# Where the Strassen weight factors of a down projection are made: in its own stage, or ahead of it and kept in DRAM

## The chip, the cores and the metric

The kernel runs on one core of a Trainium2 chip. The metric is device time in microseconds (us); with one core the slowest core is that core. Three runs of the kernel before gave 1456.2, 1456.57 and 1451.91 us, a median of 1456.2 us.

## What is computed

One step of one decoder layer on 1056 tokens (1024 of a prompt, 32 of eight decode sequences) of 1024 features, in float32. Two token mixers with four heads each come first (an mLSTM and an HGRN2), then an output projection, then a gated feed-forward part and a final norm. The change touches the feed-forward part only:

```python
D_FF = -(-8 * D_MODEL // (3 * 256)) * 256        # 2816
...
x = x + jnp.einsum('btm,md->btd', mix, w_out)
h2 = _rmsnorm(x, norm_ffn)
ff = jax.nn.silu(jnp.einsum('btd,df->btf', h2, w_gate)) * jnp.einsum('btd,df->btf', h2, w_up)
x = x + jnp.einsum('btf,fd->btd', ff, w_down)
...
y_prompt = _rmsnorm(xp, norm_final)
y_sample = _rmsnorm(xs, norm_final)
```

## The kernel before, in words

**Products.** Every float32 matrix product is made of three TensorE (PE) products of parts. An operand is cut into hi (its float32r rounding, a copy by ScalarE, ACT) and lo (the operand minus hi, a subtraction by VectorE, DVE, or GpSimd, POOL). The three products are hi hi, hi lo and lo hi.

**Stages.** After the mixers and the output projection, the feed-forward part has 22 feature tiles of 128. Tiles 0 and 1 are done plainly. The other 20 go through the seven products P1 to P7 of Strassen and Winograd. In the **gate and up products** (line 1229, about 746 to 1162 us of the span) there are 20 units u, each a gate or an up matrix for a pair of feature tiles. A unit has seven steps, a step two column halves j of 12 products with a moving operand of 264 columns. The results are summed by DVE, sent through silu by ACT, multiplied, and stored to a DRAM tensor d_ff (g_store, line 1210). The **plain part** of the down projection (line 1476) follows, to 1185 us, and then the **down stage** proper (d_step, line 1435): five chunks of four feature tiles, and in each chunk four groups, 20 groups g in all. A group is for a pair of output tiles and has seven steps of two times 6 products. After each six, DVE adds the PSUM bank to the output X in SBUF (line 1439). The final norm overlaps with the last chunk.

**Operands of the down stage.** The moving operands of a chunk (B11, T1, T2, B21, B22, T3, T4) are made from d_ff while the chunk before is multiplied (stage1, stage2): loads into three `rg` buffers, sums on DVE (lines 1299 to 1325), casts on ACT (1281), and lo subtractions of 528 columns on POOL (1282). The weights of a group are made by dsplit while the group before is multiplied. A load of 512 KB brings a raw block of `wd` into a `raw` buffer. DVE makes S1 to S4 as four sums of 256 columns (lines 1384, 1385, 1391, 1392). ACT casts, and POOL subtracts for lo, three times with 512 columns and once with 256 (line 1380; for two groups near the end DVE does it). The results go to a ring of five `whi` and five `wlo` buffers.

**What sets the order.** The program is in a hand-written order. Work beside the products is written as generators, and each emitted block of six products calls `hook()`, which counts every generator's wait down by one and runs those that are due. `yield 4` means: go on four hooks later. Each engine and each DMA queue then works through its own instructions in that order. All loads and stores that matter here are issued by one queue, SP's, where a transfer that waits (for a buffer, or for data that is to be stored) holds up those written behind it. In the gate and up products the factors of the gate and up weights are made in the same way by gsplit: sums of 512 columns on DVE (line 1146), casts on ACT (1157), lo on POOL (1158).

**PSUM in a gate or up unit.** The steps come in the order P5(u), P6(u), P1(u+1), P7(u), P2(u+1), P4(u), P3(u). P4 adds to the bank that P7 has left, so DVE must have read P7's result before P4 starts, with P2(u+1) in between. P7 in the same way needs ACT's copy of P6's result, with P1(u+1) in between.

Of the kernel before, what the change touches and what calls it, by code (L numbers as in the profile page):

```python
# [28 lines left out]
NS = 5  # L29
# [11 lines left out]
def hybrid_step(ctx: ExitStack, tc: tile.TileContext, i, o):  # L41
# [156 lines left out]
    def norm_rstd(key, n, acc, w=(2, 3)):  # L198
        """the rstd of n tokens on all partitions, from the squares summed over the feature tiles in acc"""
# [41 lines left out]
    # per-feature constants  # L241
# [7 lines left out]
    def conv_consts():  # L249
        # half the convolution and half the output gate: y sigmoid(y) = (y/2) (tanh(y/2) + 1)  # L250
# [17 lines left out]
    # ---- mLSTM gates  # L268
# [127 lines left out]
    # ---- mLSTM  # L396
# [93 lines left out]
    def norm_cols(s, sqs, nch, d2=None, p=128):  # L490
        """s = (sqs / 128 + EPS * d2) ** -0.5"""
# [108 lines left out]
    def sample_core(h_off, w, vnorm, st_in, decay, out_state, n_io, d2, k_scale, later=None):  # L600
        """the decode sequences of one head group: four heads x 32 tokens on the partitions"""
# [126 lines left out]
    # ---- HGRN2  # L728
# [174 lines left out]
    # ------------------------------------------------------------------ unit list  # L903
# [37 lines left out]
    # output projection; the token order from here on: 1024 prompt tokens, 32 decode tokens  # L941
# [62 lines left out]
    # feed-forward, first NPLAIN feature tiles  # L1004
# [36 lines left out]
    # feed-forward, the other feature tiles: pairs of them (rows of A) times two halves of the tokens (columns of B), the  # L1041
    # contraction in two halves: the seven products of Strassen and Winograd
# [21 lines left out]
    def t_prep():  # L1064
        """T1 = B12 - B11, T2 = B22 - T1, T3 = B22 - B12, T4 = B21 - T2"""
# [46 lines left out]
    WLW, DS0 = (14, 10), 1  # L1112
    DSL, DSM = {"P1": 0, "P2": 1, "P7": 2}, {"P1": 3}
# [23 lines left out]
    def gsplit(g, u, dve=False):  # L1137
        """the factors of the products: A11 A12 | S1 = A21 + A22, S2 = S1 - A11 | S3 = A11 - A21, A22 | S4 = A12 - S2"""
# [52 lines left out]
    def g_out(u, r, th, j, ps, other=None, op=None):  # L1191
        """row tile r, token half th, columns j: ps or ps + other is there"""
# [54 lines left out]
    # down projection: NS times four feature tiles in the same way (the contraction in two pairs of tiles, pairs of output  # L1247
    # tiles, halves of the tokens), the last two tiles plainly
# [3 lines left out]
    def memb(r):  # L1252
        """place r of the ring of operands: hi and lo of two feature tiles, half of the tokens"""
# [18 lines left out]
    def raw_ff(c, f):  # L1272
        """the two column blocks of a feature tile: halves of the tokens, in the last chunk halves of each half"""
# [16 lines left out]
    def stage1(c):  # L1290
        """B11, T1 = B12 - B11, T2 = B22 - T1, B21"""
# [26 lines left out]
    def diffs(c, k):  # L1318
        """T3 = B22 - B12, T4 = B21 - B11 - T3"""
# [7 lines left out]
    def stage2(c):  # L1327
        """B22, T3, T4"""
# [18 lines left out]
    draw, dw = {}, {}  # L1347

    def dload(g):
        if g >= NG:  # L1350
            return
        t = draw[g] = wp.tile([128, 1024], F32, tag="raw", name="raw", bufs=NRAW)
        f = NPLAIN + 4 * (g // 4)
        src = i["wd"].rearrange("(f p) d -> p f d", p=128)[:, f:f + 4, 256 * (g % 4):256 * (g % 4) + 256]
        nc.sync.dma_start(t.rearrange("p (f c) -> p f c", c=256), src)

    def dsplit(g):
        """A11 A12 A22 | S1 = A21 + A22, S2 = S1 - A11, S4 = A12 - S2, S3 = A11 - A21"""
        while g not in draw:
            yield 5  # L1360
        r = draw[g].rearrange("p (f c) -> p f c", c=256)
        a11, a12, a21, a22 = r[:, 0:2, 0:128], r[:, 2:4, 0:128], r[:, 0:2, 128:256], r[:, 2:4, 128:256]

        def pair(j):
            # the weights of the last chunk stay: five tiles in the ring, three in free places of the other ring
            if (g, j) in WPL:
                r = WPL[g, j]
                if r == 6:
                    return t4t[0][:, 0:1024], t4t[0][:, 1056:2080]
                return HI[:, 1056 * r:1056 * r + 1024], LO[:, 1056 * r:1056 * r + 1024]  # L1370
            return [wp.tile([128, 1024], F32R, tag=t, name=t, bufs=NW) for t in ("whi", "wlo")]

        def cut2(t):
            return t.rearrange("p (f c) -> p f c", c=128)

        def put(w, o_, src):
            n = 128 * src.shape[1]
            h, lw = cut2(w[0][:, o_:o_ + n]), cut2(w[1][:, o_:o_ + n])
            nc.scalar.activation(h, src, AF.Copy)
            (nc.vector if g in PUTD else nc.gpsimd).tensor_tensor(lw, src, h.bitcast(F32), op=OP.subtract)  # L1380
        w0 = pair(0)
        put(w0, 0, r[:, :, 0:128])
        sa = cut2(stile(512))
        nc.vector.tensor_tensor(sa[:, 0:2], a21, a22, op=OP.add)  # L1384
        nc.vector.tensor_tensor(sa[:, 2:4], sa[:, 0:2], a11, op=OP.subtract)  # L1385
        dw[g, "P1"], dw[g, "P2"], dw[g, "P4"] = [[x[:, o_:o_ + 256] for x in w0] for o_ in (0, 256, 512)]
        yield 5
        w1 = pair(1)
        put(w1, 0, sa)
        sb = cut2(stile(512))  # L1390
        nc.vector.tensor_tensor(sb[:, 0:2], a12, sa[:, 2:4], op=OP.subtract)  # L1391
        nc.vector.tensor_tensor(sb[:, 2:4], a11, a21, op=OP.subtract)  # L1392
        dw[g, "P5"], dw[g, "P6"], dw[g, "P3"], dw[g, "P7"] = [[x[:, o_:o_ + 256] for x in w1] for o_ in (0, 256, 512, 768)]
        done.add(("ds1", g))
        yield 3
        put(w1, 512, sb)
        yield 1
        put(w0, 512, a22)
        start(dload_late(g + 2), ("dl", g), 6)

    PUTD = (NG - 3, NG - 2)
    WPL = {(NG - 3, 1): 4, (NG - 1, 0): 5, (NG - 1, 1): 6}

    def dload_late(g):
        dload(g)
        return
        yield
# [7 lines left out]
    def d_step(g, p):  # L1415
        """a product for a pair of output tiles, halves of the tokens; in the last chunk for two pairs, the quarters of a half"""
# [27 lines left out]
    # the first NPLAIN feature tiles of the down projection plainly  # L1444
# [50 lines left out]
    def facc(acc, sq, dve, wait=0):  # L1495
        """a generator: acc += sq"""
# [8 lines left out]
    def squares(h):  # L1505
        """the first four tiles, half h of the tokens"""
# [14 lines left out]
    def last_squares(m, q):  # L1521
        """the last four tiles of a quarter, as they are done"""
# [48 lines left out]
    def final_half():  # L1571
        """the first half of the tokens"""
# [20 lines left out]
    # ------------------------------------------------------------------ emission  # L1593
# [88 lines left out]
    for ui, u in enumerate(units + [None]):  # L1682
        if ui == units1:
            start(t3_prep(), ("t3",))
            gi, TPK = 2, 2
            for k, (gu_, p) in enumerate(steps):
# [25 lines left out]
            for m in range(KT):  # L1712
                if m == 0:
                    dload(0)
                    dload(1)
                    load_x2(4)
                    load_x2(6)
                if m == DS0:
                    start(dsplit(0), ("ds", 0))
# [6 lines left out]
            for k, (sl, g, p) in enumerate(dsteps):  # L1726
                c, s_ = g // 4, sl % 28
                need = (g,) if g < LC else (2 * g - LC, 2 * g - LC + 1) if g < LC + 2 else ()
                if p == "P1":
                    for x in need:  # L1730
                        finish(("ds1", x))
                    if g % 4 == 0:
                        finish(("s1", c))
                if p == "P2":
                    for x in need:
                        finish(("ds", x))
                    if g % 4 == 0:
                        finish(("s2", c))
                if p == "P5" and g + 1 < LC:
                    start(dsplit(g + 1), ("ds", g + 1))  # L1740
                if p in DSL and g == LC - 1 or p in DSM and g == LC:
                    x = LC + (DSL[p] if g < LC else DSM[p])
                    start(dsplit(x), ("ds", x))
# [170 lines left out]
```

## Time and profile before

| | |
|---|---|
| runs | 1451.91, 1456.2, 1456.57 us |
| span of the profiled execution, first to last instruction | 1451.2 us |
| time of that execution outside the span | not shown; the fastest run is 0.7 us above the span |
| busy share of PE, DVE, ACT, POOL | 95, 62, 36, 50% |
| loads for the down stage | `rg<-d_ff` 42 times 528 KB, `raw<-in_wd` 22 times 512 KB |
| mean DMA rate over the span | 95 GB/s |

The profile is of one execution, with times in us. PE is TensorE, DVE VectorE, ACT ScalarE, POOL GpSimd, SP the queue that issues DMAs. A name as `S<-raw` is output and input of an instruction by the program's names, and L1384 is line 1384 of the kernel before. A busy PE is not a PE at its peak, because matmuls are pipelined and their ends modelled; a better measure is the number of products in a stretch of time. A GB/s is 10^9 bytes a second, a KB 1024 bytes.

### The profile page before, as it was taken

What the parts mean: (1) busy time and instruction counts of PE and PEld (TensorE: products, weight loads), DVE (VectorE), ACT (ScalarE), POOL (GpSimd) and SP (SyncE); (2) the same over time, 40 slices, a digit from 0 to 9 for tenths busy, and PEclk for the clock granted to TensorE, in tenths of its full rate; (3) what the DMA queues carried; (4) which work ended last, traced back from release to release, by engine and by line L of the source; (5) the groups of instructions that cost most, each with busy time, mean ns of one, the idle gap of its engine ahead of it and who ended that gap; (6) DMA issues with size and microseconds to landing.
All of it is one profiled execution on the core that took longest, in us unless ns stands there. A gap on an engine that the chain in (4) does not pass through costs nothing. (4 is left out here: it accounts for less than half of the span.)

```text
span 1451.2 us, 26916 instructions
## 1 busy us (share of the span) xinstructions
PE 1376.6 (95%) x10384; PEld 1339.6 (92%) x10384; DVE 904.0 (62%) x2120; ACT 528.8 (36%) x1195; POOL 731.9 (50%) x720
## 2 busy tenths in 40 slices
PE   7879999999999999999989999999999999998886
PEld 7769999999999998899989999999999998888885
DVE  7876657666776767745472233233322389999986
ACT  6554433322222223223344343333334423333343
POOL 5313213234343435223456655656555778888854
PEclk9989999999999999999999999999999999999998
DMA  6012212320010114443542222222212563334303
GB/s 216 22 42 76 64 37 86 109 79 29 33 44 18 44 32 133 142 148 119 182 139 74 82 89 89 69 72 89 89 64 69 182 235 134 134 134 145 123 30 121
DMA packets 85833, 138.54 MB, mean 95 GB/s; under 512 B 8240, under 2 KB 61000, under 8 KB 85192
## 3 DMA queue, kind: packets, MB, share of 16 engines
q1 hardware_dynamic: 85272, 136.57, 28.7%
q8 instruction: 82, 1.34, 0.4%
q14 instruction: 47, 0.39, 0.1%
q10 hardware_dynamic: 432, 0.24, 0.1%
HBM read 107.03 MB, written 29.75 MB: 94 GB/s over the span
## 5 line engine op out<-in xcount | busy, mean ns | idle before, releaser
L135 PE MATMUL mm<-HI,whi 128*128 128x384 f32 (+2 forms) x1160 | 382.7, 330 | 6.9 <-ACT gA L302 2.9
L137 PE MATMUL mm<-HI,wlo 128*128 128x384 f32 (+2 forms) x1160 | 363.8, 314 | 1.3 <-POOL wlo L97 1.3
L136 PE MATMUL mm<-LO,whi 128*128 128x384 f32 (+2 forms) x1160 | 363.9, 314 | 0.7 <-DVE LO L961 0.4
L135 PEld LDWEIGHTS mm<-HI,whi 128*128 128x128 f32 x1160 | 222.2, 192 | 12.2 <-ACT gA L302 3.2
L136 PEld LDWEIGHTS mm<-LO,whi 128*128 128x128 f32 x1160 | 222.4, 192 | 1.7 <-DVE LO L961 0.6
L137 PEld LDWEIGHTS mm<-HI,wlo 128*128 128x128 f32 x1160 | 221.9, 191 | 1.8 <-POOL wlo L97 1.8
L97 POOL TENSOR_TENSOR wlo<-raw,whi 128x512 fp32r<-128x512 f32 x90 | 119.7, 1339 | 144.1 <-ACT whi L96 99.2
L1158 POOL TENSOR_TENSOR wlo<-S,whi 128x512 fp32r<-128x512 f32 x78 | 107.0, 1373 | 87.1 <-ACT whi L1157 85.8
L1229 PE MATMUL mx<-T,whi 128*128 128x264 f32 x640 | 118.2, 284 | 0.0
L1229 PEld LDWEIGHTS mx<-T,whi 128*128 128x128 f32 x640 | 99.0, 188 | 0.0
L802 POOL TENSOR_TENSOR ck<-ck,wib 128x192 f32<-128x192 f32 (+2 forms) x72 | 41.2, 572 | 100.6 <-PE mx L757 56.2
L1229 PE MATMUL mx<-HI,whi 128*128 128x264 f32 x320 | 91.0, 284 | 0.0
L1229 PE MATMUL mx<-T,wlo 128*128 128x264 f32 x320 | 90.9, 284 | 0.0
L1229 PE MATMUL mx<-HI,wlo 128*128 128x264 f32 x320 | 90.9, 284 | 0.0
L1229 PE MATMUL mx<-LO,whi 128*128 128x264 f32 x320 | 90.7, 283 | 0.0
L1282 POOL TENSOR_TENSOR LO<-rg,HI 128x528 fp32r<-128x528 f32 x52 | 78.4, 1514 | 10.5 <-ACT HI L1281 5.8
L1435 PE MATMUL mx<-HI,whi 128*128 128x264 f32 x208 | 62.3, 300 | 9.9 <-DVE X L1439 9.9
L1157 ACT ACTIVATE whi<-S 128x512 fp32r<-128x512 f32 x80 | 50.2, 629 | 58.4 <-DVE S L1146 58.4
L1229 PE MATMUL mm<-HI,wlo 128*128 128x264 f32 x240 | 68.2, 284 | 0.0
L1229 PE MATMUL mm<-HI,whi 128*128 128x264 f32 x240 | 68.2, 284 | 0.0
L1229 PE MATMUL mm<-LO,whi 128*128 128x264 f32 x240 | 67.9, 283 | 0.0
L1439 DVE TENSOR_TENSOR X<-X,mx 128x264 f32<-128x264 f32 x160 | 60.7, 418 | 8.2 <-PE mx L1435 8.2
(544 smaller groups left out, 3751.8 us busy)
## 6 DMA issues: line engine op xcount, KB each, us to landing
rg<-d_ff SPq DMA_DIRECT2D x42, 528.0 KB
raw<-in_wA SPq DMA_DIRECT2D x31, 512.0 KB
raw<-in_wgu SPq DMA_DIRECT2D x24, 512.0 KB
raw<-in_wd SPq DMA_DIRECT2D x22, 512.0 KB
d_ff<-sg SPq DMA_DIRECT2D x40, 264.0 KB
rg<-in_wgu SPq DMA_DIRECT2D x20, 512.0 KB
d_h<-X SPq DMA_DIRECT2D x4, 1056.0 KB
X<-d_x SPq DMA_DIRECT2D x4, 1056.0 KB
```

Source lines behind the costliest of these rows:

```text
L97: (nc.gpsimd if pool else nc.vector).tensor_tensor(lo[:, s], raw[:, s], hi[:, s].bitcast(F32), op=OP.subtract)
L135: nc.tensor.matmul(ps[:, :n], wh, rh[:, k, :], start=(k == 0), stop=False)
L136: nc.tensor.matmul(ps[:, :n], wh, rl[:, k, :], start=False, stop=False)
L137: nc.tensor.matmul(ps[:, :n], wl, rh[:, k, :], start=False, stop=(k == nk - 1))
L802: nc.gpsimd.tensor_tensor(ke, ke, gv[:, :, 1:2].to_broadcast([128, nb, lv]), op=OP.mult)
L1157: nc.scalar.activation(hi[:, s], t, AF.Copy)
L1158: (nc.vector if dve else nc.gpsimd).tensor_tensor(lo[:, s], t, hi[:, s].bitcast(F32), op=OP.subtract)
L1229: nc.tensor.matmul(ps[:, :QN], a[:, w], b_[:, kk, c], start=new and kk == 0 and x == 0, stop=kk == 3 and x == 2, skip_group_check=True)
L1282: (nc.vector if dve else nc.gpsimd).tensor_tensor(lw, src, h.bitcast(F32), op=OP.subtract)
L1435: nc.tensor.matmul(ps[:, :QN], a[:, w], b_[k][:, cs], start=new and k == 0 and x == 0, stop=k == 1 and x == 2, skip_group_check=True)
L1439: nc.vector.tensor_tensor(y, y, ps[:, :QN], op=OP.add)
```

## The change

The weight factors of the down projection no longer come into being in the down stage. A new generator, wd_prep, is started at step (1, P1) of the gate and up products. For each of the 20 groups it loads the raw block into a new buffer `fr`, makes S1 to S4 in place on DVE, and makes hi and lo of four pieces in three new buffers `fh` (cast on ACT, lo on DVE, not on POOL). Each finished piece is stored to a new DRAM tensor d_wf. The pieces are 0 (A11, A12), 1 (A22), 2 (S2, S4) and 3 (S3, S1); piece 1 is 256 KB with hi and lo, the others 512 KB. In the down stage dload brings the ready pieces into the `whi`, `wlo` and `raw` buffers: pieces 0, 3 and 2 of group g + 2 at step P1 of group g, piece 1 of group g + 1 at step P6. The last group's pieces, and one of the group before it, go to free places of the ring of moving operands. dsplit and its DVE, ACT and POOL work in the down stage are gone. The compiler option for the DMA scratch space is made smaller, which frees SBUF; no DMA here is issued by GpSimd.

```diff
+    d_wf = dram.tile([NG, 4, 128, 1024], F32, name="d_wf")
+    def wd_prep():
+        def fload(g):
+            t = fpool[0].tile([128, 4, 256], F32, tag="fr", name="fr", bufs=1)
...
+            nc.sync.dma_start(t, i["wd"].rearrange("(f p) d -> p f d", p=128)[:, f:f + 4, 256 * (g % 4):256 * (g % 4) + 256])
+            return t
+        def piece(g, k, src):
+            n = 128 * src.shape[1]
+            t = fpool[0].tile([128, 1024], F32R, tag="fh", name="fh", bufs=3)
+            h, lw = (x.rearrange("p (f c) -> p f c", c=128) for x in (t[:, 0:n], t[:, n:2 * n]))
+            nc.scalar.activation(h, src, AF.Copy)
+            nc.vector.tensor_tensor(lw, src, h.bitcast(F32), op=OP.subtract)
+            return lambda: nc.sync.dma_start(d_wf[g, k, :, 0:2 * n], t[:, 0:2 * n].bitcast(F32))
+        r = fload(0)
+        yield WDY[0]
+        for g in range(NG):
...
+            put = piece(g, 0, left)
+            yield WDY[1]
+            put()
+            put = piece(g, 1, a22)
+            nc.vector.tensor_tensor(a22, a21, a22, op=OP.add)
+            nc.vector.tensor_tensor(a21, a11, a21, op=OP.subtract)
+            yield WDY[1]
+            put()
+            nc.vector.tensor_tensor(a11, a22, a11, op=OP.subtract)
+            nc.vector.tensor_tensor(a12, a12, a11, op=OP.subtract)
+            put = piece(g, 2, left)
+            yield WDY[1]
+            put()
+            put = piece(g, 3, right)
+            yield WDY[1]
+            put()
+            if g + 1 < NG:
+                r = fload(g + 1)
+            yield WDY[2]
+    WDY = (2, 4, 7)
...
-    def dsplit(g):
...
-            nc.scalar.activation(h, src, AF.Copy)
-            (nc.vector if g in PUTD else nc.gpsimd).tensor_tensor(lw, src, h.bitcast(F32), op=OP.subtract)
...
+    def dload(g, ks):
...
+        for k in ks:
+            t = dplace(g, k)
+            n = 256 if k == 1 else 512
+            nc.sync.dma_start(t[:, 0:2 * n].bitcast(F32), d_wf[g, k, :, 0:2 * n])
...
@@ emission @@
+                if (gu_, p) == (1, "P1"):
+                    start(wd_prep(), ("wd",))
...
-                    dload(0)
-                    dload(1)
+                    finish(("wd",))
+                    dload(0, (0, 3, 2, 1))
                     load_x2(4)
                     load_x2(6)
...
+                    dload(1, (0, 3, 2))
...
+                if p == "P1" and g + 2 < NG - 1:
+                    dload(g + 2, (0, 3, 2))
+                if p == "P6" and g + 1 < NG - 1:
+                    dload(g + 1, (1,))
+                if p == "P5" and g == LC:
+                    dload(NG - 1, range(4))
...
-                if p == "P5" and g + 1 < LC:
-                    start(dsplit(g + 1), ("ds", g + 1))
```

Line numbers in the changed program differ a little from those before: its d_step adds at line 1446, its gsplit sums at 1145, its sums of d_ff at 1298 to 1324, its new casts at 1364, lo subtractions at 1365, sums at 1376 to 1381, stores at 1366 and loads of ready pieces at 1410.

How instructions move, at three places. First DVE in the middle of the gate and up products (S and `u`, `nt`, `sg` are sums and results of a unit; x2 is a count), before:

```order
L1146 TENSOR_TENSOR S<-S,raw 128x512
L1202 TENSOR_TENSOR u_8577<-mx,u_8577 128x264
L1202 TENSOR_TENSOR u_8591<-mx,u_8591 128x264
L1196 TENSOR_TENSOR sg<-mx,nt 128x264 x2
L1146 TENSOR_TENSOR S<-raw 128x512
L1200 TENSOR_TENSOR sg<-sg,mx 128x264 x2
```

and the same place of a unit now:

```order
L1145 TENSOR_TENSOR S<-S,raw 128x512
L1365 TENSOR_TENSOR fh<-fr,fh 128x256
L1376 TENSOR_TENSOR fr<-fr 128x2x128
L1377 TENSOR_TENSOR fr<-fr 128x2x128
L1201 TENSOR_TENSOR u_9656<-mx,u_9656 128x264
L1201 TENSOR_TENSOR u_9670<-mx,u_9670 128x264
L1380 TENSOR_TENSOR fr<-fr 128x2x128
L1381 TENSOR_TENSOR fr<-fr 128x2x128
L1365 TENSOR_TENSOR fh<-fr,fh 128x512
L1195 TENSOR_TENSOR sg<-mx,nt 128x264 x2
L1365 TENSOR_TENSOR fh<-fr,fh 128x512
L1145 TENSOR_TENSOR S<-raw 128x512
```

Eight new DVE instructions a group stand between those that read PSUM banks (`mx`). Second, SP's queue at the start of the down part, before (`X<-d_x` brings in the residual, one row a pair of tiles):

```order
L1210 DMA d_ff<-sg 128x528 x2
L1355 DMA raw<-in_wd 128x4x256 x2
L1344 DMA X_12892<-d_x 128x2112 x2
L1210 DMA d_ff<-sg 128x528
L1275 DMA rg<-d_ff 128x1056 x2
```

and now:

```order
L1209 DMA d_ff<-sg 128x528 x2
L1410 DMA whi<-d_wf 128x1024 x2
L1410 DMA wlo<-d_wf 128x1024
L1410 DMA raw<-d_wf 128x512
L1343 DMA X_13333<-d_x 128x2112 x2
L1410 DMA whi<-d_wf 128x1024
L1410 DMA wlo<-d_wf 128x1024 x2
L1209 DMA d_ff<-sg 128x528
L1274 DMA rg<-d_ff 128x1056 x4
```

Seven loads of ready pieces stand where two loads of raw blocks stood, four of them ahead of the residual and all ahead of the next loads of d_ff. Third, DVE in one group of the down stage, before:

```order
L1384 TENSOR_TENSOR S<-raw 128x256
L1385 TENSOR_TENSOR S<-S,raw 128x256
L1439 TENSOR_TENSOR X_12892<-X_12892,mm 128x264
L1439 TENSOR_TENSOR X_12892<-X_12892,mx 128x264 x4
L1391 TENSOR_TENSOR S<-raw,S 128x256
L1392 TENSOR_TENSOR S<-raw 128x256
L1439 TENSOR_TENSOR X_12892<-X_12892,mm 128x264
L1439 TENSOR_TENSOR X_12892<-X_12892,so 128x264
```

and now:

```order
L1446 TENSOR_TENSOR X_13333<-X_13333,mm 128x264 x2
L1446 TENSOR_TENSOR X_13333<-X_13333,mx 128x264 x4
L1446 TENSOR_TENSOR X_13333<-X_13333,mm 128x264
L1446 TENSOR_TENSOR X_13333<-X_13333,so 128x264
```

The sums S are gone from between the additions to X; on POOL the lo subtractions of line 1380 are gone in the same way.

## Rows read from the trace of the kernel before

**Rows 1.** The page's slices, 40 equal ones of 36 us: busy tenths

```profile
PE   7879999999999999999989999999999999998886
...
DVE  7876657666776767745472233233322389999986
...
POOL 5313213234343435223456655656555778888854
```

**Rows 2.** Busy time by stretch: columns named in the first row, (x) counts instructions

```profile
core 0: us, PE busy (x) PEld busy (x) DVE busy (x) ACT busy (x) POOL busy (x), PEclk, DMA share, GB/s
800.00:1100.00 300.00, 300.00 (x2474) 300.00 (x2473) 92.54 (x161) 113.02 (x250) 174.23 (x147) 1.00 0.25 80
1160.00:1185.00 25.00, 25.00 (x163) 25.00 (x163) 21.03 (x35) 5.96 (x11) 20.02 (x18) 1.00 0.84 304
1185.00:1410.00 225.00, 201.37 (x1528) 192.30 (x1527) 218.82 (x386) 79.08 (x144) 181.69 (x132) 0.98 0.35 118
1410.00:1452.00 42.00, 28.72 (x215) 26.33 (x213) 24.76 (x55) 14.15 (x27) 19.45 (x16) 0.84 0.29 104
```

**Rows 3.** The same of the down stage's products alone, line 1435

```profile
1185.00:1410.00 225.00, 200.99 (x1524) 192.08 (x1525) 0.98 0.35 118
...
1410.00:1438.00 28.00, 21.57 (x158) 20.22 (x156) 0.95 0.21 79
```

**Rows 4.** What line 1435's engine waited for: us in all, times

```profile
  DVE X L1439: 47.9, 58
```

**Rows 5.** DVE's groups from 1200 to 1360: count | busy us, mean ns

```profile
L1439 DVE TENSOR_TENSOR X<-X,mx 128x264 f32<-128x264 f32 x104 | 38.7, 416 | 1.1 <-PE mx L1435 1.1
...
L1384 DVE TENSOR_TENSOR S<-raw 128x256 f32<-128x256 f32 x13 | 16.4, 1258 | 0.0
...
L1302 DVE TENSOR_TENSOR rg<-rg 128x528 f32<-128x528 f32 x8 | 10.8, 1354 | 0.0
```

**Rows 6.** Timeline of POOL and DVE at 1235: start, duration, engine, instruction

```profile
1235.41 1.76 POOL L1380 TENSOR_TENSOR wlo<-raw,whi 128x512 fp32r<-128x512 f32 x1
...
1235.94 1.51 DVE L1384 TENSOR_TENSOR S<-raw 128x256 f32<-128x256 f32 x1
...
1237.13 2.97 POOL L1282 TENSOR_TENSOR LO<-rg,HI 128x528 fp32r<-128x528 f32 x2
```

**Rows 7.** Single instructions of the down stage: minimum/median/maximum ns

```profile
L1384 DVE TENSOR_TENSOR S<-raw x20: 410/1208/1558, 1168.6 to 1395.4; 128x256 f32<-128x256 f32 x20
...
L1380 POOL TENSOR_TENSOR wlo<-raw,whi x34: 730/1240/1759, 1169.5 to 1377.1; 128x512 fp32r<-128x512 f32 x17, 128x256 fp32r<-128x256 f32 x17
L1380 POOL TENSOR_TENSOR wlo<-S,whi x34: 1282/1304/1754, 1173.7 to 1375.9; 128x512 fp32r<-128x512 f32 x34
...
L1282 POOL TENSOR_TENSOR LO<-rg,HI x52: 1315/1500/1832, 1155.0 to 1392.0; 128x528 fp32r<-128x528 f32 x52
...
L1325 DVE TENSOR_TENSOR rg<-rg x10: 693/1447/1706, 1182.7 to 1388.2; 128x528 f32<-128x528 f32 x10
```

**Rows 8.** The same in the gate and up products

```profile
L1158 POOL TENSOR_TENSOR wlo<-S,whi x78: 1281/1302/1747, 758.3 to 1144.4; 128x512 fp32r<-128x512 f32 x78
...
L1203 POOL TENSOR_TENSOR sg<-sg,u x40: 743/757/1216, 791.7 to 1167.0; 128x264 f32<-128x264 f32 x40
...
L1146 DVE TENSOR_TENSOR S<-raw x20: 680/681/1604, 741.2 to 1122.6; 128x512 f32<-128x512 f32 x20
...
L1146 DVE TENSOR_TENSOR S<-S,rg x10: 1662/1664/1668, 763.1 to 1129.9; 128x512 f32<-128x512 f32 x10
```

**Rows 9.** Two stretches with much DMA: the last columns are DMA share and GB/s

```profile
1165.00:1177.00 12.00, 12.00 (x77) 12.00 (x76) 10.99 (x17) 3.27 (x6) 10.97 (x10) 1.00 1.01 388
900.00:906.00 6.00, 6.00 (x51) 6.00 (x51) 2.76 (x5) 2.67 (x6) 3.18 (x3) 1.00 0.69 223
```

**Rows 10.** What SP's queue waited for from 800 to 1150: us, times, longest

```profile
SPq L1210 <- POOL sg L1203: 229.0, 26, 14.6
```

**Rows 11.** ACT at the end of the plain part, timeline

```profile
1178.71 0.65 ACT L1281 ACTIVATE T<-rg 128x528 fp32r<-128x528 f32 x1 [2.29 <-DMA rg<-d_ff]
```

More of the change, by code (lines that the diff above doesn't have):

```diff
@@ L1111, in hybrid_step @@
     GSK = 11
-    WLW, DS0 = (14, 10), 1
-    DSL, DSM = {"P1": 0, "P2": 1, "P7": 2}, {"P1": 3}
+    WLW = (14, 10)
     def t3_prep():
@@ L1346, in hybrid_step @@
     NG = 4 * NS
-    draw, dw = {}, {}
-    def dload(g):
+    dw = {}
+    d_wf = dram.tile([NG, 4, 128, 1024], F32, name="d_wf")
+    def wd_prep():
+        def fload(g):
+            t = fpool[0].tile([128, 4, 256], F32, tag="fr", name="fr", bufs=1)
+            f = NPLAIN + 4 * (g // 4)
+            nc.sync.dma_start(t, i["wd"].rearrange("(f p) d -> p f d", p=128)[:, f:f + 4, 256 * (g % 4):256 * (g % 4) + 256])
[10 more added lines that the diff above has]
+        for g in range(NG):
+            left, right = r[:, :, 0:128], r[:, :, 128:256]
+            a11, a12, a21, a22 = left[:, 0:2], left[:, 2:4], right[:, 0:2], right[:, 2:4]
+            put = piece(g, 0, left)
[17 more added lines that the diff above has]
+            yield WDY[2]
@@ L1350, in dload, with dplace @@
+    WDY = (2, 4, 7)
+    def dplace(g, k):
+        if (g, k) in WPL:
+            r, j = WPL[g, k]
+            if r == 6:
+                return t4t[0][:, 1056 * j:1056 * j + 1024]
+            return (HI, LO)[j][:, 1056 * r:1056 * r + 1024]
+        tag = ("whi", "raw", "wlo", ("whi", "wlo")[g % 2])[k]
+        return wp.tile([128, 1024], F32R, tag=tag, name=tag, bufs=NRAW if tag == "raw" else NW)
+    def dload(g, ks):
         if g >= NG:
             return
-        t = draw[g] = wp.tile([128, 1024], F32, tag="raw", name="raw", bufs=NRAW)
@@ L1353, in dload @@
-        f = NPLAIN + 4 * (g // 4)
-        src = i["wd"].rearrange("(f p) d -> p f d", p=128)[:, f:f + 4, 256 * (g % 4):256 * (g % 4) + 256]
-        nc.sync.dma_start(t.rearrange("p (f c) -> p f c", c=256), src)
-    def dsplit(g):
[L1359 to L1378, printed above, removed]
-            nc.scalar.activation(h, src, AF.Copy)
-            (nc.vector if g in PUTD else nc.gpsimd).tensor_tensor(lw, src, h.bitcast(F32), op=OP.subtract)
[L1381 to L1407, printed above, removed]
+        for k in ks:
+            t = dplace(g, k)
+            n = 256 if k == 1 else 512
+            nc.sync.dma_start(t[:, 0:2 * n].bitcast(F32), d_wf[g, k, :, 0:2 * n])
+            for x, p in enumerate((("P1", "P2"), ("P4",), ("P6", "P3"), ("P7", "P5"))[k]):
+                dw[g, p] = t[:, 256 * x:256 * x + 256], t[:, n + 256 * x:n + 256 * x + 256]
@@ L1409, in hybrid_step @@
+    WPL = {(NG - 2, 1): (4, 0), (NG - 1, 0): (4, 1), (NG - 1, 1): (5, 0), (NG - 1, 2): (5, 1), (NG - 1, 3): (6, 0)}
     DSLOT = {"P1": 0, "P5": 1, "P6": 3, "P2": 4, "P3": 5, "P7": 6, "P4": 9}
@@ L1713, in hybrid_step @@
                 if m == 0:
-                    dload(0)
-                    dload(1)
+                    finish(("wd",))
+                    dload(0, (0, 3, 2, 1))
                     load_x2(4)
                     load_x2(6)
-                if m == DS0:
-                    start(dsplit(0), ("ds", 0))
+                    dload(1, (0, 3, 2))
                 for j in range(3):
@@ L1727, in hybrid_step @@
                 c, s_ = g // 4, sl % 28
[L1728 to L1738, printed above, removed]
-                if p == "P5" and g + 1 < LC:
-                    start(dsplit(g + 1), ("ds", g + 1))
-                if p in DSL and g == LC - 1 or p in DSM and g == LC:
-                    x = LC + (DSL[p] if g < LC else DSM[p])
-                    start(dsplit(x), ("ds", x))
+                if p == "P1" and g % 4 == 0:
+                    finish(("s1", c))
+                if p == "P2" and g % 4 == 0:
+                    finish(("s2", c))
+                if p == "P1" and g + 2 < NG - 1:
[4 more added lines that the diff above has]
+                    dload(NG - 1, range(4))
                 if p == "P2" and g % 4 == 0 and c + 1 < NS:
@@ L1902 @@
     from concourse.bass_utils import run_bass_kernel_spmd as _run
-    nc = _bacc.Bacc("TRN2", target_bir_lowering=False, num_devices=1)
+    nc = _bacc.Bacc("TRN2", target_bir_lowering=False, num_devices=1, dynamic_dma_scratch_size=2048)
     arrays = {"in_" + k: np.ascontiguousarray(v) for k, v in _prepare(inputs).items()}
```

## The prediction

> **What bounds the kernel now.** I read the 40 slices first, to see where PE is not full. PE is at nine tenths nearly everywhere, and DVE is at nine tenths from slice 33 on, which is the down stage, after two to four tenths in the gate and up products; POOL rises to eight there [rows 1]. Then busy time by stretch. From 800 to 1100 us, inside the gate and up products, PE is never idle and does 2474 products in 300 us, so a product takes 0.1213 us at full rate; DVE is busy 31% and POOL 58% [rows 2]. From 1185 to 1410 us the granted clock is 0.98, DVE is busy 218.8 of 225 us, and the down stage does 1524 products [rows 2, 3]. At the full rate these take 1524 x 0.1213 = 184.8 us, so **40 us are lost** there. Line 1435 waited 47.9 us, in 58 waits, for DVE's addition to X [rows 4], that is for a PSUM bank to be read. After 1410 the 158 last products take 28 us where 19 would do; DVE's final-norm work stands there too, and I leave these 9 us as they are.
>
> **Why DVE is full.** Additions to X, with one operand in PSUM, take 416 ns; a sum of only 256 columns with both operands in SBUF takes 1258 ns on average [rows 5], yet 410 ns at best [rows 7]. The timeline shows why: POOL starts a lo subtraction at 1235.41 for 1.76 us; DVE's sum issued at 1235.94 ends at 1237.45, after POOL's end at 1237.17, and POOL's next ones begin at 1237.13 [rows 6]. So I read that a DVE instruction with two SBUF operands and a POOL instruction exclude each other, and that each one's best time is its price alone. A group's share of this common path, by the minima of rows 7: POOL 3 x 1.282 + 0.730 = 4.6 us (weights) and 3.5 x 1.315 = 4.6 us (14 lo subtractions of moving operands a chunk), DVE 4 x 0.41 = 1.6 us (weight sums) and 2.5 x 0.69 = 1.7 us (ten sums a chunk of d_ff). The sum is 12.5 us. A group is 84 products, and 225 us / (1524 / 84) is 12.4 us measured, against 84 x 0.1213 = 10.2 us of PE. The common path of DVE and POOL sets the pace.
>
> **What the change removes.** In the down stage 4.6 + 1.6 us a group leave this path; 6.3 of 10.2 us remain. DVE keeps 14 additions, 14 x 0.416 = 5.8 us, and 2.5 sums of 0.69 to 1.35 us [rows 5, 7], 7.6 to 9.2 us in all, under PE's 10.2. ACT loses work only. So PE becomes the bound and up to 40.2 us come back. What could remain lost in the steady part is bounded by 0 and by DVE at 9.2 of 10.2 us with unlucky order, say half of today's loss, 20 us. The nearest row is the plain part, where DVE is busy 21 of 25 us, POOL 20, and PE loses nothing [rows 2]; I take 2.
>
> **What it adds to the down stage: DMA.** A group's pieces are 1792 KB (1.84 MB) in place of 512, and two d_ff tiles of 528 KB (1.08 MB) stay, 2.92 MB per 10.2 us or 286 GB/s. The queue has moved 388 GB/s at a full DMA share, for 12 us [rows 9]. That is 74%, and the pieces are asked for two groups (20 us) ahead. At the start it is tighter: these 12 us of full share are where the seven new loads come, and they bring 3.41 MB for 1.05, so the queue runs 2.36 MB / 388 GB/s = 6 us longer. The residual is delayed by 2 us, which the banks bridge. The d_ff tiles behind the pieces, which ACT already awaits at 1178.7 us [rows 11], land near 1185. DVE's sums on them stand between the plain part's last additions. Between 0 and 6 us, I take 2. In the last chunk the groups 18 and 19 are needed at once, 3.41 MB, 8.8 us at that rate, within seven steps of 1.46 us: 0 to 4 us, I take 1.
>
> **What it adds to the gate and up products.** Twenty rounds of 4 x 4 + 7 = 23 hooks of six products, 16.7 us each, 335 us in all, from about 765 to 1100 us, well before the stage ends at 1162; nothing is left over for the down stage to finish. Each round puts four ACT casts (about 0.6 us each, on an engine that is 38% busy), five DVE operations of 256 and three of 512 columns, one load and four stores into the queues. On the common path there are now, in a unit of 168 products (20.4 us), ten POOL operations, 7 x 1.281 + 3 x 0.743 = 11.2 us, and four sums, 4 x 0.68 = 2.7 us [rows 8], 68%. The new DVE work is 5 x 0.41 + 3 x 0.68 = 4.1 us per 16.7 us, a further 25%: **93%**. That is nearly full where it was easy, but not over. DVE's busy time goes from 31% to between 56% (prices alone) and 99% (1.66 us for each 512 and 1.26 us for each 256, as when POOL is met [rows 5, 8]). PE notices only if a bank is read late. The tightest ones are P7's (DVE) and P6's (ACT): three half steps of 12 products, 4.4 us, less 0.4 for the reading, so DVE may be 3.9 us late. The DVE work written between two bank reads is at most some 4 us when POOL is met. So the bounds are 0 and, if it went as in today's down stage at a DVE share of 97%, a loss of 40 / 225 = 18% of 335 us, 60 us. The plain part (DVE 84%, no loss) is again nearer than the down stage: I take **5**.
>
> The Trainium skill, "SBUF — State Buffer", section "Who interferes with whom", has a rule that speaks against moving this work here: a DVE instruction with two SBUF inputs and a GpSimd one that reads SBUF lock each other out for the whole instruction, and the one that starts first wins, so nothing favours the one PE needs. Without such a lock the gate and up products would have DVE at 56% and cost 0; with it they are the 93% above. Rows 6 agree with the rule.
>
> **Sum.** -40.2 + 2 + 2 + 1 + 5 = -30 us. The page shows no time beside the span of 1451.2 us, so I use the fastest run, 1451.9, which is 0.3% (4.3 us) below the median of 1456.2: **1422 us**.
>
> **Rivals.**
> *The gate and up products give it back.* The queues are in order and coupled. ACT's cast of a piece waits for the store of the piece three before (three `fh` buffers); that store is issued after DVE's late lo subtraction and behind d_ff stores that wait for POOL, on which SP's queue already waits 229 us [rows 10]; from the issue 8 hooks, 5.8 us, remain, while a 512 KB transfer at 223 GB/s takes 2.3 us. If ACT then stands still beyond 3.9 us, PE stops. The point of decision: at 35 / 20 = 1.75 us a round the gain is gone. At 0.75 to 1.75 us a round the time is 1432 to 1452; at 3 us a round, 1451.9 - 35 + 60 = **1477**, slower. For it: 93% and four engines in order. Against: PE has no wait at all in this stage now, and a late PE delays the hooks too, so the load gives way.
> *DMA bounds the down stage.* Six microseconds in the gate and up products moved only 223 GB/s at a share of 0.69 [rows 9]. If single loads with waits between them do no better, a group takes 2.92 MB / 223 = 13.1 us, 0.7 more than now: 18 x 0.7 + 5 + 2 more, **1472**; at 250 GB/s, 11.7 us, still 1446. Against: rows 9 have 388 GB/s when several transfers are queued, as they are here. The same page of the Trainium skill, section "A bandwidth-pool intuition that's wrong", calls HBM almost always the end-to-end bottleneck, not SBUF, which speaks against a round trip through DRAM to relieve an SBUF path. Its 358 GB/s a core gives an estimate of 8.2 us a group, under PE's 10.2, and the trace of before contradicts the rule: DMA share 0.35 while PE waits for DVE.
> *DVE stays near the bound in the down stage*, because sums wait for late d_ff tiles and additions stand behind them: half the loss stays, 1452 - 20 + 8 = 1440.
>
> **Chances.** Forecast, with the gate and up products costing at most 15 us: 0.66, own range 1407 to 1437 (all terms at 0 and a few us of the tail, to 15 us more). Half gains (DVE stays, or 0.75 to 1.5 us a round): 0.15, 1435 to 1447. Gain just eaten: 0.07. Slower by the gate and up products 0.08, by DMA 0.04. So faster by over 0.3% (what a measurement of this kernel can tell) 0.81, within it 0.07, slower 0.12. The range 1407 to 1450 leaves out the slower cases and little below.
>
> **What would show it.** Right: in the gate and up products PE still has about 825 products per 100 us, with DVE at 55 to 90%; in the down stage a group takes 10.2 to 10.6 us, line 1446 waits for DVE under 8 us, the sums that remain take under 1.1 us, and the DMA share is 0.7 to 0.8. Wrong: PE waits for ACT's u or nt or DVE's sg in the gate and up products, over 15 us in all; ACT waiting on DMA for `fh`; PE waiting in the down stage for weight loads. Under 1407 would mean that the tail shrank too.

## The result, and the profile after

| | before | after |
|---|---|---|
| runs of this comparison, median (lowest to highest), us | 1455.05 (1451.91 to 1456.57), 5 runs | 1445.37 (1442.34 to 1449.3), 5 runs |
| span of the profiled execution | 1451.2 | 1440.5 |
| first product of the plain part, in the span | 1162.4 | 1186.8 |
| first and last product of the down stage | 1185.4 and 1437.4 | 1209.8 and 1427.1 |

The ratio is 0.9936, with an interval of 0.9918 to 0.9955: faster, by about 9 us where 30 were forecast. (The profiled run took 1442.34 us, 1.8 us more than its span.) The third and fourth lines tell where the difference lies. The plain part starts **24.4 us later**, so the stages before it, in which only the gate and up products were changed, have become that much longer (the gate and up products start at 746.0 us, before at 746.1). The plain part takes 23.0 us as it did. The down stage takes 217.3 us in place of 252.0, **34.7 us less**. The rest takes 13.4 us for 13.8. So the change does what it says in the down stage, and two thirds of that are lost in the stage to which the work was moved.

The page's slices of the kernel after, in tenths, against [rows 1]:

```profile
PE   7879999999999998999988998999999999999996
DVE  7876657666777768744564655656555436777776
```

DVE is no longer at nine tenths in the down stage (slices 33 on), and it does four to six tenths in the gate and up products (slices 21 to 30, counted from 0), where it did two to three. PE now has an eight in slices 21 and 24, where it had nines.

Busy time by stretch, against [rows 2] (columns as there), of all engines, and then of line 1442's products alone, against [rows 3]:

```profile
800.00:1100.00 300.00, 284.99 (x2294) 282.49 (x2294) 174.14 (x283) 132.58 (x298) 165.32 (x136) 0.98 0.60 207
...
1187.00:1412.00 225.00, 221.85 (x1769) 220.58 (x1768) 165.76 (x346) 52.15 (x85) 103.89 (x78) 1.00 0.73 266
```

```profile
1210.00:1400.00 190.00, 187.12 (x1529) 186.13 (x1528) 1.00 0.74 271
```

In the down stage 1529 products take 190 us, 0.124 us each at a granted clock of 1.00, where 225 us were needed for 1524 before. That is 10.4 us for a group of 84. DVE is busy 166 of 225 us, DMA at a share of 0.74. In the gate and up products PE did 2294 products in the 300 us in which it did 2474 before; at 0.1213 us the 180 missing ones are 21.8 us. PE is idle for 15.0 us of these, and the granted clock is 0.98 in place of 1.00, which is some 6 us more.

What line 1442's engine waited for in the whole stage, against the 47.9 us of [rows 4], which are of the whole stage too (us, times; L1485 adds the plain part's products to X):

```profile
  DVE X L1446: 5.9, 8
  DVE X L1485: 3.3, 3
```

What PE's weight loads waited for from 760 to 1160 us (us in all, times, longest), where no such wait was there before:

```profile
PEld mx L1228 <- DVE sg L1195: 7.3, 5, 3.7
PEld mx L1228 <- DVE u L1201: 6.7, 3, 5.5
PEld mx L1228 <- ACT u L1236: 6.3, 7, 1.6
```

The weight loads stand for 20.3 us, the products behind them for 17.2 us in the same waits. The lower clock after the stops makes up the rest of the 24 us. PE waits for a bank to be read, of the 20.3 us 14.0 for DVE and 6.3 for ACT. So what kept DVE and ACT? The same view for ACT and DVE:

```profile
ACT fh L1364 <- issue: 31.4, 9, 5.5
ACT fh L1364 <- DMA fr<-in_wd: 30.0, 11, 5.9
...
DVE fh L1365 <- ACT fh L1364: 129.3, 72, 8.5
```

ACT's first cast of a round waits for the load of the raw block, `fr`, in 11 rounds of 20 by name. Of the nine waits that the view gives to "issue", six are also before the first cast of a round, 4.6 to 7.4 us after the load was asked for, and three before a later piece, whose sums stand behind the late ones on DVE. One stop of the first kind, first SP's queue, then ACT, DVE, and PE's weight loads (start, duration, engine, instruction, idle time before it and what ended it):

```profile
872.52 0.38 SPq L1366 DMA_DIRECT2D d_wf<-fh  x1
872.96 0.42 SPq L1357 DMA_DIRECT2D fr<-in_wd  x1
...
880.39 0.63 ACT L1364 ACTIVATE fh<-fr 128x512 fp32r<-128x512 f32 x1 [5.46 <-issue]
...
881.05 0.69 DVE L1365 TENSOR_TENSOR fh<-fr,fh 128x512 fp32r<-128x512 f32 x1 [7.83 <-ACT fh L1364]
883.35 1.28 DVE L1365 TENSOR_TENSOR fh<-fr,fh 128x256 fp32r<-128x256 f32 x1 [1.00 <-ACT fh L1364]
884.67 1.37 DVE L1376 TENSOR_TENSOR fr<-fr 128x256 f32<-128x256 f32 x1
886.41 0.76 DVE L1201 TENSOR_TENSOR u<-mx,u 128x264 f32<-128x264 f32 x2
...
886.89 0.50 PEld L1228 LDWEIGHTS mx<-T,whi 128*128 128x128 f32 x2 [5.48 <-DVE u L1201]
```

The load is asked for at 872.96, when the round before has been cast, since there is one `fr` buffer. In the written order the cast comes seven hooks of six products later, about 5.1 us of PE's work. That is a distance in the program, not a time that ACT leaves the load: ACT has nothing else written ahead of the cast and has stood at it since 874.93. The data are there only at 880.39, 7.4 us after the request. DVE, whose next instruction is that piece's lo subtraction, has stood for 7.83 us by then. It has the rest of the round before it, too, and reads the bank that PE needs at 886.41. PE stood for 5.48 us. The DMA share from 872 to 879 us was 0.91, at 291 GB/s, so 2.0 MB or nearly four blocks of 512 KB moved in these 7 us: the load stood behind a round's last stores and two loads of the gate and up weights.

The request hangs on DVE, too. Ahead of it in SP's queue stands the store of the round's last piece, which needs DVE's last lo subtraction. In 15 of the 19 rounds after the first, the request goes out 0.4 us after that subtraction ends, in the other four 2.1 to 2.2 us after it. One of the 15, where the subtraction ends at 946.19:

```profile
944.84 1.35 DVE L1365 TENSOR_TENSOR fh<-fr,fh 128x512 fp32r<-128x512 f32 x1 [1.22 <-ACT fh L1364]
946.22 0.32 SPq L1366 DMA_DIRECT2D d_wf<-fh  x1
946.59 0.43 SPq L1357 DMA_DIRECT2D fr<-in_wd  x1
951.00 0.63 ACT L1364 ACTIVATE fh<-fr 128x512 fp32r<-128x512 f32 x1 [1.75 <-DMA fr<-in_wd]
```

So a round in which DVE is late also asks late for the next block.

### The profile page after: what moved, and what is told of

It reads as the page before. It is cut to its first block, busy times and chain, and to the rows that moved or that the text cites. A ratio compares the mean times of both kernels' runs of the same rounds, so it can differ in the third digit from the quotient of the medians.

```text
span 1440.5 us, 27183 instructions
## 1 busy us (share of the span) xinstructions
PE 1366.2 (95%) x10384; PEld 1334.2 (93%) x10384; DVE 930.2 (65%) x2192; ACT 523.5 (36%) x1195; POOL 636.8 (44%) x648
## 5 line engine op out<-in xcount | busy, mean ns | idle before, releaser
L1365 DVE TENSOR_TENSOR fh<-fr,fh 128x512 fp32r<-128x512 f32 x80 | 71.6, 894 | 129.4 <-ACT fh L1364 129.3
L1157 POOL TENSOR_TENSOR wlo<-S,whi 128x512 fp32r<-128x512 f32 x78 | 103.2, 1328 | 115.9 <-ACT whi L1156 109.0
L1228 PE MATMUL mx<-T,whi 128*128 128x264 f32 x640 | 122.6, 290 | 12.4 <-DVE sg L1195 6.3
L1281 POOL TENSOR_TENSOR LO<-rg,HI 128x528 fp32r<-128x528 f32 x52 | 70.5, 1365 | 65.7 <-ACT HI L1280 65.7
L1228 PE MATMUL mx<-HI,whi 128*128 128x264 f32 x320 | 91.7, 287 | 4.8 <-ACT u L1236 4.8
L1446 DVE TENSOR_TENSOR X<-X,mx 128x264 f32<-128x264 f32 x160 | 65.3, 424 | 27.1 <-PE mx L1442 26.6
L1364 ACT ACTIVATE fh<-fr 128x512 fp32r<-128x512 f32 x80 | 45.6, 572 | 71.5 <-issue 31.4
L1280 ACT ACTIVATE HI<-rg 128x528 fp32r<-128x528 f32 x52 | 32.3, 641 | 105.7 <-PE mx L1442 32.8
```

The source lines that it names most:

```text
L1157: (nc.vector if dve else nc.gpsimd).tensor_tensor(lo[:, s], t, hi[:, s].bitcast(F32), op=OP.subtract)
L1228: nc.tensor.matmul(ps[:, :QN], a[:, w], b_[:, kk, c], start=new and kk == 0 and x == 0, stop=kk == 3 and x == 2, skip_group_check=True)
L1281: (nc.vector if dve else nc.gpsimd).tensor_tensor(lw, src, h.bitcast(F32), op=OP.subtract)
L1365: nc.vector.tensor_tensor(lw, src, h.bitcast(F32), op=OP.subtract)
L1446: nc.vector.tensor_tensor(y, y, ps[:, :QN], op=OP.add)
```

## The experiments

The reading above is **theory A**: the raw block's load comes too late, because with one buffer the request stands only 5.1 us of PE's work ahead of the cast, and the queue needs more. Its rivals are **B**: DVE and POOL cannot both use their common path at a load of 93% without PE being late (the prediction's own worry), and **C**: the order is at fault, since DVE's lo subtraction is written right behind ACT's cast, so that any lateness of ACT holds DVE's bank reads. Four kernels ran together, beside a kernel before of 1454.23 us (median of 7 runs).

**Two `fr` buffers**, the load asked for a whole round ahead; to make room, two large `fh` buffers and a small one in place of three large ones:

```diff
-            t = fpool[0].tile([128, 4, 256], F32, tag="fr", name="fr", bufs=1)
+            t = fpool[0].tile([128, 4, 256], F32, tag="fr", name="fr", bufs=2)
...
-            t = fpool[0].tile([128, 1024], F32R, tag="fh", name="fh", bufs=3)
+            t = fpool[0].tile([128, 2 * n], F32R, tag="fh" if n > 256 else "fh1", name="fh", bufs=2 if n > 256 else 1)
...
-        r = fload(0)
+        nxt_r = fload(0)
...
+            r = nxt_r
+            if g + 1 < NG:
+                nxt_r = fload(g + 1)
...
-            if g + 1 < NG:
-                r = fload(g + 1)
```

> The changed kernel with two fr buffers, so that the raw block of a group is asked for a whole round (23 hooks, 16.7 us) before its first cast in place of 7 hooks (5.1 us); the fh buffer of piece 1 is cut to its size to make room. Theory A, late load: the gate and up products lose 24 us because ACT stands at the first cast of a round for a load that needs 4.4 to 7.5 us behind other transfers. Then ACT's waits for fr fall from about 61 us to under 10, the gate and up products lose under 9 us, and the time falls by 12 to 20 us below the changed kernel, to 1425 to 1433. Theory B, the common path of DVE and POOL is too full (93%): the same work stands on it, the loss stays at 20 us or more, 1441 to 1447. Theory C, DVE waits in order for ACT's casts (129 us): part of the loss stays, 1433 to 1441.

Measured: 1422.71 us, a ratio of 0.9773 (0.9751 to 0.9794) to before. The time is 2 us under theory A's range. The plain part starts at 1166.5, 4.1 us after the kernel before in place of 24.4; 1.7 of these lie ahead of the gate and up products, which start at 747.9 in this execution. What ACT's casts wait for from 760 to 1160 us is now

```profile
ACT fh L1364 <- DVE fr L1384: 14.2, 11, 5.2
ACT fh L1364 <- issue: 7.7, 2, 5.0
ACT fh L1364 <- DMA fr<-in_wd: 5.2, 1, 5.2
```

The load is waited for once, in the first round; the two "issue" waits are before later pieces. The 61 us of the last two rows are 13, and some 20 of the 24 us went with the late load.

**The same buffer, more time** (ten hooks from the request to the first cast, not seven):

```diff
-    WDY = (2, 4, 7)
+    WDY = (2, 4, 10)
```

> The changed kernel with 10 hooks in place of 7 between the request of a raw block and its first cast, so 7.3 us of reserve and rounds of 26 hooks. Theory A: most waits for the load go, the loss in the gate and up products falls from 24 to about 10 us, 1429 to 1436. Theory B: the path's load falls only from 93 to 90%, 1440 to 1446. Theory C: nearly no change, 1440 to 1446.

Measured: 1424.92 us, 0.9792 (0.9771 to 0.9813), better than expected. Three hooks more, 2.2 us, do nearly what a buffer does; ACT still waits for the load six times, 13.5 us, and PE starts the plain part at 1169.0. This run has the buffers of the change, but 90% on the common path; the run before has the 93% of the change, but other `fh` buffers. What both share is more time between the request and the cast.

**The lo subtraction two hooks after its cast**, with the load as late as in the change:

```diff
-            nc.vector.tensor_tensor(lw, src, h.bitcast(F32), op=OP.subtract)
-            return lambda: nc.sync.dma_start(d_wf[g, k, :, 0:2 * n], t[:, 0:2 * n].bitcast(F32))
+            return lambda: nc.vector.tensor_tensor(lw, src, h.bitcast(F32), op=OP.subtract), lambda: nc.sync.dma_start(d_wf[g, k, :, 0:2 * n], t[:, 0:2 * n].bitcast(F32))
...
-            put = piece(g, 0, left)
-            yield WDY[1]
+            low, put = piece(g, 0, left)
+            yield 2
+            low()
+            yield 2
             put()
```

and the same for the other pieces.

> The changed kernel with each lo subtraction of DVE written two hooks after ACT's cast of its piece, and not right behind it. Theory A: ACT still waits for the load, and P6's copy on ACT with it; DVE no longer stands behind ACT, so some of the stops go, 1437 to 1444. Theory B: the same work on the path, 1441 to 1447. Theory C: the loss falls by half or more, 1428 to 1436, and DVE's waits for fh fall from 129 us to under 40.

Measured: 1429.82 us, 0.9831 (0.981 to 0.9853). The waits from 760 to 1160 us:

```profile
DVE fh L1365 <- ACT fh L1364: 75.0, 40, 7.7
ACT fh L1364 <- issue: 42.6, 14, 5.1
ACT fh L1364 <- DMA fr<-in_wd: 30.3, 10, 5.6
```

ACT waits for the load as in the change, 30.3 us by name for 30.0, and in both six of the "issue" waits, 18.9 us, are before a round's first cast. Yet 15 of the kernel's us are back. So A and C are not rivals but links of one chain: the load is late, and DVE, in order behind ACT, carries that to PE. Either link may be opened. DVE's own wait fell to 75 us only, not as far as C had it.

**Both at once:**

> Both: two fr buffers and the lo subtraction two hooks after the cast. Theory A: as the two buffers alone, 1424 to 1432. Theory C: a further gain of 5 us or more over the two buffers alone. Theory B: 1441 to 1447.

Measured: 1417.62 us, 0.9747 (0.9727 to 0.9767). That is 5.1 us under the two buffers alone, as theory C had it, though the two intervals overlap. The gate and up products, from their first product to the plain part's, take 415.3 us, for 416.3 in the kernel before, 418.7 with two buffers alone and 440.7 in the change: they carry the moved work at no cost. From 800 to 1100 us:

```profile
800.00:1100.00 300.00, 300.00 (x2473) 300.00 (x2473) 202.52 (x305) 145.29 (x322) 184.45 (x149) 1.00 0.63 220
```

PE is busy throughout with 2473 products (2474 before), while DVE does 202 us and POOL 184. The work on the common path is the same as in the change, and denser, so **B falls**: a load of 93% by itself does not make PE late.

Four more ran beside a kernel before of 1451.18 us (median of 7).

**The cost without the gain:** the kernel before with the preparation added at its place, and the down stage left as it was, so that nothing reads the prepared pieces:

```diff
@@ in the kernel before @@
+                if (gu_, p) == (1, "P1"):
+                    start(wd_prep(), ("wd",))
...
+                    finish(("wd",))
                     dload(0)
                     dload(1)
```

> One part alone: the kernel before, its down stage as it was, with the new work in the gate and up products (loads, casts, lo subtractions, stores) added; nothing reads what it stores. If the parts add, as the stages of the two traces say (+24 us in the gate and up products, -35 us in the down stage), the time is 24 us above the kernel before, 1474 to 1482. If the loss in the gate and up products came from something in the changed down stage, or the added work cost little by itself (my 5 us), it is 1456 to 1464.

Measured: 1477.62 us, 1.0181 (1.0154 to 1.0207), that is 26 us slower; the plain part starts at 1189.8, 27.4 us later, and the down stage takes 253.4 us for 252.0. The parts add: -35 in the down stage and about +26 here make the 9 us that the change gains, within the noise. The smaller DMA scratch space is in this run, too, and the down stage shows no effect of it.

**What makes the load late:** the pieces of group 0 alone are stored (4 of 80 stores), and the down stage reads them for every group.

```diff
-            return lambda: nc.sync.dma_start(d_wf[g, k, :, 0:2 * n], t[:, 0:2 * n].bitcast(F32))
+            return (lambda: None) if g else (lambda: nc.sync.dma_start(d_wf[g, k, :, 0:2 * n], t[:, 0:2 * n].bitcast(F32)))
...
-            nc.sync.dma_start(t[:, 0:2 * n].bitcast(F32), d_wf[g, k, :, 0:2 * n])
+            nc.sync.dma_start(t[:, 0:2 * n].bitcast(F32), d_wf[0, k, :, 0:2 * n])
```

> The changed kernel with 4 of its 80 stores to d_wf: only group 0's pieces are stored, and the down stage loads these 20 times, in the same sizes and places; so the weights of groups 1 to 19 in the result are those of group 0. Theory A1, the load of the raw block is late because it stands in the queue behind this generator's own stores: ACT's waits for it fall from 61 us to under 20 and the time to 1424 to 1432. Theory A2, it is late because of the gate and up loads of 1 MB and the blocks' short rows: the waits stay over 40 us and the time is 1437 to 1446.

Measured: 1428.44 us, 0.9834 (0.9816 to 0.9853). Busy time by stretch, and the waits from 760 to 1160 us:

```profile
800.00:1100.00 300.00, 295.73 (x2425) 294.46 (x2424) 187.18 (x300) 141.07 (x316) 180.80 (x148) 1.00 0.35 111
```

```profile
ACT fh L1364 <- DVE fr L1381: 21.7, 13, 5.2
ACT fh L1364 <- DMA fr<-in_wd: 21.4, 12, 4.9
```

The DMA share falls from 0.60 to 0.35 and 15 of the kernel's us come back, as theory A1 has it, but ACT's waits for the load, 21.4 us in 12 times, stay a little over the 20 that A1 allowed. From the request to the cast it is now 3.6 to 4.8 us in 14 of the 20 rounds, for 4.4 to 7.5 with the stores. So the change's own stores make most of the lateness, by their bytes or by their own wait for DVE in the queue; this run does not part the two. The rest isn't shown to be the gate and up loads: the request is now held by DVE directly, since it needs the one `fr` buffer, and goes out 0.03 us after the round's last lo subtraction ends in 14 of 19 rounds.

**More on the common path:** the kernel with both mends, with the lo subtractions on POOL, where one of 512 columns takes 1.28 us at best [rows 8] in place of 0.68 on DVE:

```diff
-            return lambda: nc.vector.tensor_tensor(lw, src, h.bitcast(F32), op=OP.subtract), lambda: nc.sync.dma_start(d_wf[g, k, :, 0:2 * n], t[:, 0:2 * n].bitcast(F32))
+            return lambda: nc.gpsimd.tensor_tensor(lw, src, h.bitcast(F32), op=OP.subtract), lambda: nc.sync.dma_start(d_wf[g, k, :, 0:2 * n], t[:, 0:2 * n].bitcast(F32))
```

> The kernel with two fr buffers and later lo subtractions (1417.6 us), with these 80 subtractions on POOL and not on DVE. Theory L, POOL and DVE with two SBUF operands share one path and their best times are its price: the new work then has 4 x 0.41 + 3 x 1.28 + 0.73 = 6.2 us of 16.7 a round, 37%, with the 68% of the unit's own work 105%. The gate and up products then lose at least 5% of 335 us, 17 us: 1433 to 1460. Theory M, each engine has its own load (POOL 58 + 27 = 85%, DVE 31 + 10 = 41%): no loss, 1415 to 1422.

Measured: 1438.11 us, 0.9903 (0.988 to 0.9925), some 20 us more than without this edit; the gate and up products take 434.6 us for 415.3. The stretch, and PE's waits from 760 to 1160 us:

```profile
800.00:1100.00 300.00, 289.74 (x2343) 288.06 (x2344) 132.74 (x221) 135.19 (x306) 247.64 (x208) 0.99 0.60 209
```

```profile
PEld mx L1228 <- ACT u L1236: 8.1, 4, 3.0
PEld mm L1228 <- ACT nt L1236: 7.4, 2, 7.1
PEld mx L1228 <- DVE sg L1195: 3.1, 2, 2.4
PEld mx L1228 <- DVE u L1201: 3.0, 3, 2.6
```

The path's load, worked out as in the prediction, rises by (3 x 0.60 + 0.33) us in 16.7, from 93 to about 105%, and the loss is in the range expected of that. This agrees with the lock of the Trainium skill, "SBUF — State Buffer", section "Who interferes with whom"; but it isn't shown by this alone. The in-place sums on DVE also stand behind POOL's subtractions now (88.8 us of waits), and ACT's casts wait five times for a store to free their `fh` buffer (9.8 us).

**The start of the down part:** in the kernel with both mends, piece 1 of group 0 and the pieces of group 1 are asked for in the middle of the plain part, behind the residual and the first d_ff tiles, not ahead of them:

```diff
-                    dload(0, (0, 3, 2, 1))
+                    dload(0, (0, 3, 2))
                     load_x2(4)
                     load_x2(6)
-                    dload(1, (0, 3, 2))
+                if m == 4:
+                    dload(0, (1,))
+                    dload(1, (0, 3, 2))
```

> The same base (1417.6 us), with the loads of group 1's pieces and of group 0's piece 1 asked for after four of the eight output tiles of the plain part, behind the loads of d_ff that DVE waits for. If the 2.4 us that PE waits at the start of the down stage come from these d_ff tiles standing behind the weights, as the trace says, 1414 to 1416.5; if not, 1416.5 to 1420.

Measured: 1414.01 us, 0.9728 (0.9705 to 0.9752), the fastest of all. In its trace the down stage takes 213.2 us, for 218.4 without this edit. 25 us from about its first product on, without the edit and then with it:

```profile
1183.00:1208.00 25.00, 22.78 (x171) 22.46 (x171) 20.58 (x44) 7.03 (x12) 14.96 (x11) 0.93 0.75 275
```

```profile
1187.00:1212.00 25.00, 25.00 (x206) 25.00 (x205) 20.42 (x48) 7.42 (x12) 16.61 (x12) 1.00 0.88 323
```

PE does 206 products where it did 171, at a clock of 1.00 for 0.93. The two intervals of the whole time overlap, so the gain, 2.8 us by the two ratios, is seen in the trace rather than in the runs.

## Why the prediction was wrong, and where it was right

**The down stage: right.** The terms -40.2 + 2 + 2 + 1 came to -35.2; measured are -34.7. The common path of DVE and POOL was the bound, and PE is the bound without the 6.2 us a group: 10.4 us a group were measured, in the 10.2 to 10.6 foretold, at a DMA share of 0.74 in the 0.7 to 0.8, and with few waits for additions to X. The terms agree in place, too. From 1210 to 1400 us, the start and the steady part, 1529 products at 0.1213 us are 185.5 us of the 190, so 4.5 us are lost for 2 + 2 in the sum. Of these, waits of 1.65 and 0.87 us are at the start, behind DVE, whose first sum sat for 4.57 us for a d_ff tile. After 1400 us about 9.4 us are lost, where 9 were left as they were and 1 was added. A detail was wrong without harm: the sums that remain were to take under 1.1 us, and one of the five lines still takes twice its best of 693 ns [rows 7]:

```profile
L1324 DVE TENSOR_TENSOR rg<-rg x10: 1398/1500/1716, 1212.0 to 1380.0; 128x528 f32<-128x528 f32 x10
```

DVE, busy 166 of 225 us, has time for it.

**DMA as the bound of the down stage, and DVE staying near it: rightly held unlikely.** 271 GB/s were moved, near the 286 worked out, and no wait of PE's for a ready piece shows in the stage.

**The gate and up products, "I take 5": wrong, 24.** This is the step that failed. The term was taken from the load of a resource, 93% of the common path, and from the plain part as the nearest row. That load alone was no cause: at the same load the two mends bring the term to zero. What cost was one transfer that came late, and an order of instructions that passed this on to DVE and PE. The prediction had the right kind of danger in its first rival (engines in order, PE stopped once ACT stands still), and the result, 24.4 / 20 = 1.2 us a round, lies in that rival's middle band. Of the signs named for it, PE did 765 products per 100 us, not 825; its waits for ACT's u and DVE's sg came to 13.6 us, under the 15 named, and with those for DVE's u, not named, to 20.3. But the prediction looked at the wrong transfer and with the wrong price. It counted the reserve of the `fh` stores, 5.8 us, against 2.3 us for 512 KB at 223 GB/s, a transfer alone, and ACT never waits for such a store in the change's gate and up products. Of the raw block's load it said only "one load". That one has a single buffer and 5.1 us of reserve by the same count, and takes 4.4 to 7.5 us in the queue. An estimate of what can stand ahead of it would have shown the danger: two stored pieces and two weight blocks, 512 KB each, and its own are five times 1.35 us at the 388 GB/s of [rows 9], 6.8 us, if none of them has moved yet. This is the case of the worst rounds, as the stop shown with its 7.4 us; 13 of the 20 rounds take 4.4 to 5.5. The prediction's point against, that a late PE delays the hooks too so that the load gives way, was of no help in the stop shown: DVE had two lo subtractions, two of the group's sums and one of the gate and up weights' to catch up on before it read PE's bank.

The sum of -30 us is near what the moved work gives once the load is in time: 31.5 us less with two buffers. That the two times, 1422 and 1422.71, agree so closely is chance, since the forecast starts from the fastest run, 1451.9, and the other is measured beside a kernel before of 1454.23. The chance of 0.15 for half a gain was too small next to 0.66.

## What to carry to other kernels

When work is moved into a stage with idle engines, list each wait that it brings into an in-order engine, and compare the reserve of the transfer behind it with all bytes that stand ahead of it in the queue at that moment, the moved work's own stores first. Ask as well what the request itself waits for. A second buffer, or a few more steps between request and use, gave back most of the loss here, with the same work on the engines. And write an operation that needs another engine's result some steps after that result, not right behind it: then a late transfer that stops the one engine does not at once stop the other.

## What was not expected of the hardware

- A path worked out to be 93% full cost PE nothing over 300 us (2473 products, clock 1.00), as long as the bank reads were not held behind a late transfer. At a load worked out as 105% the kernel lost 20 us, though with other waits in it, as said above.
- A stop costs more than its own length. Around the stop shown, in windows of 5 us of all engines:

```profile
880.00:885.00 5.00, 1.61 (x14) 1.41 (x12) 2.91 (x4) 2.09 (x4) 1.91 (x2) 0.97 0.26 105
885.00:890.00 5.00, 3.11 (x14) 3.11 (x15) 4.19 (x7) 1.08 (x3) 2.39 (x3) 0.50 0.26 99
890.00:895.00 5.00, 5.00 (x37) 5.00 (x37) 3.12 (x8) 2.64 (x8) 1.28 (x1) 0.85 0.37 150
895.00:900.00 5.00, 5.00 (x43) 5.00 (x42) 1.91 (x3) 1.98 (x5) 4.94 (x5) 1.00 0.96 248
```

  PE stands from 881.4 to 886.9. Then the granted clock is 0.50, the 1.2 GHz level, and it is back at 1.00 after 895. By the timeline 101 products begin in the 20 us (the rows above count one that reaches over a border in both); full rate would be 165, so the stop of 5.5 us costs 64 x 0.1213 = 7.8.
- The change's own runs spread over 7 us (1442.34 to 1449.3), those of the kernel with both mends over 4 (1416.86 to 1420.91). Why is open; part of it may lie ahead of the change, since the first gate or up product starts anywhere from 745.6 to 748.6 us in the ten traces.
